# Down projection in seven block products: another order of the products, b11 loaded once, activation loads placed earlier in the program

## The chip, the cores and the metric

The kernel runs on one core of one Trainium2 chip. The metric is the device time of one execution in microseconds, the median of several runs of the same program. Each engine works through a queue of its own in order: TensorE (PE) multiplies, VectorE (DVE) and ScalarE (ACT) work on tiles, SyncE (SP) and GpSimd (POOL) issue the transfers here, POOL also adds a little. TensorE's clock can be throttled; the profile gives the clock that was granted.

## The reference

One encoder layer is applied to two requests of 256 and 512 tokens with the same weights; the kernel joins them to 768 rows. After three token mixers, a gated merge and an output projection comes the feed-forward part, in float32:

```python
    h2 = rmsnorm(x, ffn_norm_g[li])
    g, up = jnp.split(h2 @ w_gate_up[li], 2, axis=-1)
    x = x + (jax.nn.silu(g) * up) @ w_down[li]
    return x
```

`D_MODEL` is 1024 and `D_FF` 2816. The change touches only the last product, the down projection: hidden activations (768 x 2816) times `w_down` (2816 x 1024), added to the residual rows `x1` and stored.

## The kernel before

**Precision.** Each float32 operand is split in a rounded high part (written by ACT) and a low part (the rest, written by DVE). A product is three matmuls per 128-row step, `mm3` (L751 to L753): high by high, low by high, high by low. In the profile `whd` and `wld` are the parts of a weight tile, `dxh` and `dxl` those of an activation tile, and `split_evac` (L742, L743 without a scale, L745, L746 with one) writes them.

**Hidden activations.** The gate and up projections run in 11 blocks of 256 hidden columns. Block `fb` ends in an SBUF tile `fa` (128 x 1536 numbers, 0.786 MB), which SP stores to a DRAM tile `hid_scr[fb]` (L1425). The last such store, of block 10, is the last thing that the gate and up stage does.

**Seven products.** The down projection cuts rows and columns in halves: a11, a12, a21, a22 are the activations, with `A_(r, kh)` for row half `r` (384 rows each) and hidden half `kh`; b11, b12, b21, b22 are the quarters of `w_down`, `w_quarter(kh, f, g)` with `f` the half of the output columns. Seven products of sums of them give the four output blocks, in the order P1, P5, P6, P3, P7, P2, P4. P1 is a11 by b11, P2 a12 by b21. The hidden half is cut in granules `g` = 0 to 5 of two 128-row steps (the last has one). A product and a granule make an *item*, 42 in all, number 6 p + g. A full item is 3 row tiles x 2 steps x 3 matmuls = 18 matmuls, the last granule's 9; all are 693.

**Activation tiles.** `a_load` (L1712) fetches one half granule pair, 128 x 768 numbers (0.393 MB, half of that for granule 5), from `hid_scr` as `da<r><kh>_<g>`. The first `EARLY` = 3 lie in a pool of their own (`dae`) and are fetched during the gate and up stage. All others come from a pool that is opened when that stage's pools are closed and takes over their memory, so such a load waits for what is still read there, the last store of `fa` included. Sums of activations are made by DVE in place (L1757, `da` out of `da` and `da`, and `ds` for P3).

**Weight tiles.** A weight tile is 128 x 1024 numbers (0.524 MB, 0.262 for granule 5). Names in the profile: `dwr` are plain loads for P1, P3 and P2, with item numbers, in three buffers shared with the earlier stages; `dwt` are P7's, in three buffers; `dch0` to `dch5` are the *sum chain*, six tiles that stay. SP loads b11 into each, POOL adds b12 by an accumulating load (L1744) for P5, then b22 for P6, then b21 for P4, each after the splits of the item before have read the tile. P7's tile is b12 with b22 added.

**Order.** `w_fetch(i)` issues item i's weight load, `make(i)` its splits. The program runs `w_fetch` six and `make` two items ahead of the matmuls, but a list scheduler then places every instruction on its engine, so the written order is only the start. PE keeps four weight parts (`whd`, `wld`) and three activation parts (`dxh`, `dxl`). Products P1, P6, P7 and P4 gather in one set of three PSUM banks (`b`), P5 and P3, and then P2, in another (`d`). At a product's last granule DVE adds the three banks to `x1` (L1829), and after the last addition to a block SP stores it (L1831).

Of the kernel before, what the change touches and what calls it, by code (L numbers as in the profile page):

```python
# [626 lines left out]
def hybrid_block(ctx, tc, A, outs, consts):  # L627
# [20 lines left out]
    def uid(s):  # L648
        cnt[0] += 1
        return f"{s}_{cnt[0]}"  # L650
# [88 lines left out]
    def split_evac(hi, lo, src, scale=None):  # L739

        if scale is None:
            act.activation(hi, src, AF.Copy)  # L742
            v.tensor_tensor(out=lo, in0=src, in1=hi.bitcast(F32), op=sub)  # L743
        else:
            act.activation(hi, src, AF.Copy, scale=scale)  # L745
            v.scalar_tensor_tensor(out=lo, in0=src, scalar=scale, in1=hi.bitcast(F32), op0=mul, op1=sub)  # L746

    def mm3(ps, wh, wl, xh, xl, start, stop, more=False):

        kw = {"skip_group_check": True} if more else {}  # L750
        pe.matmul(ps, wh, xh, start=start, stop=False, **kw)  # L751
        pe.matmul(ps, wh, xl, start=False, stop=False, **kw)  # L752
        pe.matmul(ps, wl, xh, start=False, stop=stop, **kw)  # L753
# [43 lines left out]
    def bcast_load(pool, ap, n, name):  # L797
        t = pool.tile([128, n], F32, name=name)
        nc.sync.dma_start(t, ap.unsqueeze(0).to_broadcast([128, n]))
        return t  # L800
# [168 lines left out]
    D, P3 = {}, {}  # L969
    mrs2 = k1.tile([128, 4], F32, name="mrs2")  # L970
    with tc.tile_pool(name="nrm", bufs=1) as pool, tc.tile_pool(name="nrmg", bufs=1) as pg:
# [43 lines left out]
        g = bcast_load(pg, A["norm_mix_g"][0], 1024, "gmix")  # L1015
# [120 lines left out]
    for i, nme in enumerate(("diff_q_g", "diff_k_g")):  # L1136
        g = rp[:, 2, 64 * i : 64 * i + 64]
# [5 lines left out]
        s_ = slice(2 * i, 2 * i + 2)  # L1143
# [336 lines left out]
    with ExitStack() as c5:  # L1480
# [93 lines left out]
        g = fnp.tile([128, 1024], F32, name="gffn", bufs=1)  # L1574
# [117 lines left out]
    hid_store(0)  # L1692


    P1, P5, P6, P3, P7, P2, P4 = range(7)
    NG = NFB // 2 + 1

    def granule(kh, g):
        if g < NG - 1:
            return (NG - 1) * kh + g, 0, 2  # L1700
        return NFB - 1, kh, 1

    ITEMS = [(p, g) for p in range(7) for g in range(NG)]
    AHEAD, FETCH = 2, 6
    EARLY = 3
    de = ctx.enter_context(ExitStack())
    de.enter_context(tc.tile_pool(name="dgap", bufs=1, side="right")).tile([128, 16], F32, name="dgap")
    da_f = de.enter_context(tc.tile_pool(name="daf", bufs=3, side="right"))
# [3 lines left out]
    def a_load(q, g):  # L1712

        r, kh = q
        fb, m, n = granule(kh, g)
        early = q == (0, 0) and g < EARLY
        t = (da_e if early else DP["a"]).tile([128, 2, HT], F32, name=f"da{r}{kh}_{g}")[:, 0:n]
        nc.sync.dma_start(t, hid_scr[fb][:, m : m + n, HT * r : HT * r + HT])
        a_raw[q, g] = t

    def w_quarter(kh, f, g):
        fb, m, n = granule(kh, g)
        return wd[:, 2 * fb + m : 2 * fb + m + n, 512 * f : 512 * f + 512]

    def w_fetch(i):

        if i >= len(ITEMS):
            return
        p, g = ITEMS[i]
        n = granule(0, g)[2]  # L1730
        view = lambda t: t.rearrange("p (k c) -> p k c", k=2)[:, 0:n]
        if p in (P5, P6, P4):
            if p == P5:
                ch[g] = view(DP["ch"].tile([128, 1024], F32, name=f"dch{g}"))
                nc.sync.dma_start(ch[g], w_quarter(0, 0, g))
            t = ch[g]
            src, acc = None, {P5: (0, 1), P6: (1, 1), P4: (1, 0)}[p]
        else:
            t = view(DP["r"].tile([128, 1024], F32, name=f"dwt{i}", tag="dwt") if p == P7 else
                     W.praw.tile([128, W.HALF], F32, name=f"dwr{i}", tag="wr"))  # L1740
            src, acc = {P1: ((0, 0), None), P3: ((1, 1), None), P7: ((0, 1), (1, 1)), P2: ((1, 0), None)}[p]
            nc.sync.dma_start(t, w_quarter(*src, g))
        if acc:
            gp.dma_start(t, w_quarter(*acc, g), accum_op=add)  # L1744
        w_raw[i] = t

    def make(i):

        if i >= len(ITEMS):
            return  # L1750
        p, g = ITEMS[i]
        n = granule(0, g)[2]
        t = w_raw.pop(i)
        wh, wl = (x.rearrange("p (k c) -> p k c", k=2)[:, 0:n] for x in W.tiles(f"d{i}"))
        split_evac(wh, wl, t)
        A_ = lambda r, kh: a_raw[(r, kh), g]
        tt = lambda o, x, y, op: v.tensor_tensor(out=o, in0=x, in1=y, op=op)  # L1757
        sign = 0.5
        s_ = None if p == P1 else A_(1, 0)
        if p == P1:  # L1760
            x = A_(0, 0)
        elif p == P5:
            x = s_
            tt(x, x, A_(1, 1), sub)
        elif p == P6:
            x = s_
            tt(x, x, A_(0, 0), sub)
        elif p == P3:
            x = DP["t"].tile([128, 2, HT], F32, name=uid("ds4"), tag="ds4")[:, 0:n]
            tt(x, s_, A_(0, 1), add)  # L1770
        elif p == P7:
            x = s_
            tt(x, x, A_(1, 1), add)
            sign = -0.5
        else:
            x = A_(*((0, 1) if p == P2 else (1, 1)))
        xh, xl = (da_f.tile([128, 2, HT], F32R, name=uid("dx" + w), tag="dx" + w)[:, 0:n] for w in "hl")
        split_evac(xh, xl, x, sign)
        parts[i] = xh, xl, wh, wl

    def down_early():
        for i in range(3):
            w_fetch(i)
        for g in range(EARLY):
            a_load((0, 0), g)
        for i in range(AHEAD):
            make(i)

# [7 lines left out]
    with ExitStack() as c7:  # L1796
        for k, n in (("a", 1), ("ch", 1), ("t", 2), ("r", 3)):
            DP[k] = c7.enter_context(tc.tile_pool(name="down" + k, bufs=n))
        loads = [((0, 0), g) for g in range(EARLY, NG)]
        loads += [(q, g) for g in range(NG) for q in ((1, 0), (1, 1))] + [((0, 1), g) for g in range(NG)]  # L1800
        HOME = {P1: (0, 0, add), P5: (1, 1, add), P6: (0, 1, sub), P3: (0, 1, add), P7: (1, 1, sub),
                P2: (0, 0, add), P4: (1, 0, add)}
        acc = {}
        for _ in range(NG - EARLY):
            a_load(*loads.pop(0))
        for i in range(3, FETCH):
            w_fetch(i)
        for i, (p, g) in enumerate(ITEMS):
            for _ in range(3):
                if loads:  # L1810
                    a_load(*loads.pop(0))
            w_fetch(i + FETCH)
            make(i + AHEAD)
            bank = "b" if p in (P1, P6, P7, P4) else "d"
            if g == 0 and p in (P1, P5, P2):
                acc[bank] = [PS[bank].tile([128, 512], F32, name=uid("dn"), tag=bank) for _ in range(3)]
            ps = acc[bank]
            n = granule(0, g)[2]
            xh, xl, wh, wl = parts.pop(i)
            for t in range(3):  # L1820
                c = slice(128 * t, 128 * t + 128)
                for k in range(n):
                    mm3(ps[t], xh[:, k, c], xl[:, k, c], wh[:, k], wl[:, k],
                        g == 0 and k == 0 and p in (P1, P5, P2), g == NG - 1 and k == n - 1, p in (P6, P3, P7, P4))
            if g == NG - 1:
                r, f, op = HOME[p]
                for t in range(3):
                    o = x1[3 * r + t][:, 512 * f : 512 * f + 512]
                    v.tensor_tensor(out=o, in0=o, in1=ps[t], op=op)  # L1829
                    if p in (P3, P7, P2, P4):  # L1830
                        nc.sync.dma_start(os_[3 * r + t][:, 512 * f : 512 * f + 512], o)  # L1831
    de.close()
    x1ctx.close()
# [43 lines left out]
```

## Time and profile before

| | us |
|---|---|
| median of 3 runs | 1800.08 (1798.48 to 1800.41) |
| profiled execution | 1797.81 |
| its span, first to last instruction | 1796.0 |
| PE busy | 1742.0 (97%) |
| DVE busy | 1262.5 (70%) |
| ACT busy | 887.0 (49%) |
| POOL busy | 280.7 (16%) |

The page's 40 slices are 44.9 us each; the down projection takes the last four and a half of them. A row of the timeline reads: start, duration, engine, line, operation, output and inputs, shapes, and in brackets how long the engine stood idle before and what released it. SPq and POOL rows with DMA in them are issues, not transfers; several issues of a line are merged to one row with their count, which then spans from the first to the last. A row of the waits reads: who waited for whom, total us, times, longest. A row of the windows reads: stretch and its length, then busy time and count of PE, PE's weight loads, DVE, ACT and POOL, granted clock, busy share of the DMA engines, GB/s. DMA queue q1 carries what SP issues, q0 what POOL issues.

### The profile page before, as it was taken

To read this page: it belongs to the slowest core of one execution; us is meant where nothing else is said; L and a number is where in the kernel's file an instruction comes from. 1 tells how busy PE (TensorE), PEld (TensorE's weight loads), DVE (VectorE), ACT (ScalarE), POOL (GpSimd) and SP (SyncE) were. 2 spreads that over 40 slices of the span, in tenths; PEclk is the share of its full clock that TensorE was granted. 3 is DMA by queue.
4 is the path that set the end of the run, shared out by engine and by line. 5 is a ranking of instruction groups with operands and counts; after the bars stand their busy time and mean duration, and the time that the engine had idled before them with its cause. 6 is when DMAs were issued, how large, how long until landed. Compare 5 with 4: busy or idle time off the path is not lost.

```text
span 1796.0 us, 29428 instructions
## 1 busy us (share of the span) xinstructions
PE 1742.0 (97%) x11194; PEld 1608.4 (90%) x11194; DVE 1262.5 (70%) x2342; ACT 887.0 (49%) x1856; POOL 280.7 (16%) x300
## 2 busy tenths in 40 slices
PE   9999999999999999999989999999999999993999
PEld 8999988999999999999979888888899999982887
DVE  6665659699999588788865435443897777752964
ACT  6444444777676366787755333232444333321443
POOL 0000000000000101011100011000155555541200
PEclk9999999999999999999999999999999999996999
DMA  7223745664565566454853346331234323269851
GB/s 263 72 83 106 135 115 127 162 159 117 148 150 145 133 171 147 96 112 105 188 144 100 121 132 220 122 109 47 71 99 134 105 90 106 88 191 300 166 153 43
DMA packets 211165, 236.97 MB, mean 132 GB/s; under 512 B 57928, under 2 KB 173392, under 8 KB 211024
## 3 DMA queue, kind: packets, MB, share of 16 engines
q1 hardware_dynamic: 185584, 166.93, 30.8%
q0 software_dynamic: 24288, 65.02, 17.0%
q10 hardware_dynamic: 1152, 3.15, 0.5%
q8 instruction: 88, 1.44, 0.3%
q14 instruction: 53, 0.43, 0.1%
HBM read 168.66 MB, written 41.22 MB: 117 GB/s over the span
## 4 chain that ended last, share of the span: by engine, by line
PE 57%; DMA 4%; DVE 2%; issue 1%; SPq 1%; ACT 0%; POOL 0%; DVEq 0%; ACTq 0%; POOLq 0%
PE br L752 4%; PE br L751 4%; PE br L753 4%; PE gate L751 3%; PE gate L752 3%; PE up L752 3%; PE gate L753 3%; PE up L751 3%; PE up L753 3%; PE dn L753 3%; PE dn L751 3%; PE dn L752 3%; PE av L1311 2%; PE qk L752 2%; PE qk L751 2%; PE qk L753 2%
## 5 line engine op out<-in xcount | busy, mean ns | idle before, releaser
L595 ACT ACTIVATE wh<-wr 128x1024 fp32r<-128x1024 f32 x124 | 140.6, 1134 | 73.4 <-PE br L752 30.3
L601 DVE TENSOR_TENSOR wl<-wr,wh 128x1024 fp32r<-128x1024 f32 x82 | 108.4, 1323 | 84.4 <-ACT wh L595 82.6
L751 PE MATMUL gl<-Hhi,wh 128*128 128x256 f32 (+1 forms) x384 | 132.4, 345 | 2.3 <-ACT glt L1114 2.3
L753 PE MATMUL gl<-Hhi,wl 128*128 128x256 f32 (+1 forms) x384 | 129.0, 336 | 0.0
L752 PE MATMUL gl<-Hlo,wh 128*128 128x256 f32 (+1 forms) x384 | 128.7, 335 | 0.0
L751 PE MATMUL dn<-whd,dxh 128*128 128x512 f32 x231 | 90.8, 394 | 29.6 <-ACT dxh L745 29.6
L751 PE MATMUL qk<-wh,Hhi 128*128 128x256 f32 x384 | 108.7, 283 | 0.7 <-ACT V L1210 0.7
L752 PE MATMUL qk<-wl,Hhi 128*128 128x256 f32 x384 | 109.2, 284 | 0.0
L753 PE MATMUL qk<-wh,Hlo 128*128 128x256 f32 x384 | 108.4, 282 | 0.0
L599 POOL DMA_DIRECT2D wl<-wr x42 | 36.6, 872 | 453.9 <-ACT wl L598 440.5
L752 PE MATMUL dn<-wld,dxh 128*128 128x512 f32 x231 | 90.5, 392 | 0.0
L753 PE MATMUL dn<-whd,dxl 128*128 128x512 f32 x231 | 88.3, 391 | 1.2 <-DVE dxl L746 1.2
L751 PEld LDWEIGHTS gl<-Hhi,wh 128*128 128x128 f32 x384 | 72.3, 188 | 9.7 <-ACT glt L1114 2.7
L753 PEld LDWEIGHTS gl<-Hhi,wl 128*128 128x128 f32 x384 | 72.0, 187 | 8.0
L751 PEld LDWEIGHTS dn<-whd,dxh 128*128 128x128 f32 x231 | 43.9, 190 | 38.9 <-ACT dxh L745 30.0
L752 PEld LDWEIGHTS gl<-Hlo,wh 128*128 128x128 f32 x384 | 72.3, 188 | 7.2
L745 ACT ACTIVATE dxh<-da 128x768 fp32r<-128x768 f32 (+1 forms) x36 | 28.5, 792 | 93.9 <-PE dn L752 49.4
L751 PEld LDWEIGHTS qk<-wh,Hhi 128*128 128x128 f32 x384 | 73.1, 190 | 1.6 <-ACT V L1210 0.9
L1280 DVE TENSOR_REDUCE nm<-sc 128x1 f32<-128x512 f32 (+1 forms) x96 | 56.6, 598 | 25.5 <-PE sc L1275 24.5
L753 PEld LDWEIGHTS qk<-wh,Hlo 128*128 128x128 f32 x384 | 73.4, 191 | 0.3
L752 PEld LDWEIGHTS qk<-wl,Hhi 128*128 128x128 f32 x384 | 73.1, 190 | 0.6
L557 ACT ACTIVATE wh_S<-ws 128x512 fp32r<-128x512 f32 x70 | 41.1, 625 | 59.1 <-PE up L752 33.5
(478 smaller groups left out, 6046.6 us busy)
## 6 DMA issues: line engine op xcount, KB each, us to landing
wr<-in_w_in_dram SPq DMA_DIRECT2D x48, 512.0 KB, 4.5
wr<-in_w_gate_up_dram SPq DMA_DIRECT2D x44, 512.0 KB, 3.6
wl<-wr POOLq DMA_DIRECT2D x42, 512.0 KB, 5.4
wr<-in_w_branch_dram SPq DMA_DIRECT2D x24, 512.0 KB, 4.4
glr<-gl_scr POOLq DMA_DIRECT2D x24, 384.0 KB, 3.5
hid_scr<-fa SPq DMA_DIRECT2D x11, 768.0 KB, 6.5
wr<-in_w_mem_kv_dram SPq DMA_DIRECT2D x16, 512.0 KB, 3.6
wr<-in_w_in_dram SPq DMA_DIRECT2D x32, 256.0 KB, 4.3
```

The lines of the kernel that those rows point to most:

```text
L557: self.nc.scalar.activation(f(hi), src, AF.Copy)
L595: self.nc.scalar.activation(hi, r, AF.Copy)
L599: self.nc.gpsimd.dma_start(lo, r.bitcast(F32R), accum_op=ALU.add)
L601: self.sub.tensor_tensor(out=lo, in0=r, in1=hi.bitcast(F32), op=ALU.subtract)
L745: act.activation(hi, src, AF.Copy, scale=scale)
L751: pe.matmul(ps, wh, xh, start=start, stop=False, **kw)
L752: pe.matmul(ps, wh, xl, start=False, stop=False, **kw)
L753: pe.matmul(ps, wl, xh, start=False, stop=stop, **kw)
L1280: v.tensor_reduce(out=nm[:, m : m + 1], in_=ps, axis=AX.X, op=ALU.max, negate=True)
L1311: pe.matmul(po[:, 0:128], aT[:, 128 * k : 128 * k + 128], V[:, c0 // 128 + k, 128 * (h % 2) : 128 * (h % 2) + 128], start=(k == 0), stop=( ...
```

## The change

The products' order becomes P2, P1, P5, P6, P3, P7, P4. P1 no longer loads b11 into tiles of its own; it reads the sum chain's tile before anything is added to it, so b11 is read once and P5's addition of b12 follows P1's split. Four activation tiles, now of a12, are fetched early, where it was three of a11. The others are issued by item, seven items ahead, where a list gave three per item. P2's block is now stored after P1's addition.

```diff
-    P1, P5, P6, P3, P7, P2, P4 = range(7)
+    P2, P1, P5, P6, P3, P7, P4 = range(7)
...
-    AHEAD, FETCH = 2, 6
-    EARLY = 3
+    AHEAD, FETCH, LOAD = 2, 6, 7
+    EARLY = 4
+    NEW = {P2: ((0, 1),), P1: ((0, 0),), P5: ((1, 0), (1, 1))}
...
-        early = q == (0, 0) and g < EARLY
+        early = q == (0, 1) and g < EARLY
...
-        if p in (P5, P6, P4):
-            if p == P5:
+        acc = None
+        if p in (P1, P5, P6, P4):
+            if p == P1:
                 ch[g] = view(DP["ch"].tile([128, 1024], F32, name=f"dch{g}"))
                 nc.sync.dma_start(ch[g], w_quarter(0, 0, g))
+            else:
+                acc = {P5: (0, 1), P6: (1, 1), P4: (1, 0)}[p]
             t = ch[g]
-            src, acc = None, {P5: (0, 1), P6: (1, 1), P4: (1, 0)}[p]
...
-            src, acc = {P1: ((0, 0), None), P3: ((1, 1), None), P7: ((0, 1), (1, 1)), P2: ((1, 0), None)}[p]
+            src, acc = {P3: ((1, 1), None), P7: ((0, 1), (1, 1)), P2: ((1, 0), None)}[p]
...
+    def item_loads(i):
+        if i < len(ITEMS):
+            p, g = ITEMS[i]
+            for q in NEW.get(p, ()):
+                a_load(q, g)
...
-        for g in range(EARLY):
-            a_load((0, 0), g)
+        for i in range(EARLY):
+            item_loads(i)
...
-        loads = [((0, 0), g) for g in range(EARLY, NG)]
-        loads += [(q, g) for g in range(NG) for q in ((1, 0), (1, 1))] + [((0, 1), g) for g in range(NG)]
...
-        for _ in range(NG - EARLY):
-            a_load(*loads.pop(0))
+        for i in range(EARLY, LOAD):
+            item_loads(i)
...
-            for _ in range(3):
-                if loads:
-                    a_load(*loads.pop(0))
+            item_loads(i + LOAD)
...
-                    if p in (P3, P7, P2, P4):
+                    if p in (P1, P3, P7, P4):
```

Lines behind the change stand up to five lower in the kernel after: L1718 becomes L1719, L1744 L1747, L1757 L1760, L1829 L1834, L1831 L1836.

What the scheduler makes of it shows at three places. First SP's queue, from the last hidden store on, before:

```order
L1425 DMA hid_scr10_174<-fa_1786_17435 128x1536
L1742 DMA dwr19_18143<-in_w_down_dram 128x2x512
L1742 DMA dwr20_18172<-in_w_down_dram 128x2x512
L1718 DMA da00_3_17728<-hid_scr3_167 128x2x384
L1718 DMA da00_4_17730<-hid_scr4_168 128x2x384
L1718 DMA da00_5_17732<-hid_scr10_174 128x384
L1718 DMA da10_0_17740<-hid_scr0_164 128x2x384
L1718 DMA da11_0_17742<-hid_scr5_169 128x2x384
```

The same stretch of SP's queue after, with the six rows ahead of the store (`dwr24` to `dwr26` are P3's weights now, `dwt30` to `dwt32` P7's):

```order
L1737 DMA dch5_17899<-in_w_down_dram 128x512
L1745 DMA dwt30_18440<-in_w_down_dram 128x2x512
L1745 DMA dwr5_17740<-in_w_down_dram 128x512
L1745 DMA dwt31_18471<-in_w_down_dram 128x2x512
L1745 DMA dwt32_18502<-in_w_down_dram 128x2x512
L1425 DMA hid_scr10_174<-fa_1786_17435 128x1536
L1745 DMA dwr24_18270<-in_w_down_dram 128x2x512
L1745 DMA dwr25_18299<-in_w_down_dram 128x2x512
L1745 DMA dwr26_18328<-in_w_down_dram 128x2x512
L1719 DMA da01_4_17730<-hid_scr9_173 128x2x384
L1719 DMA da01_5_17732<-hid_scr10_174 128x384
L1719 DMA da00_0_17734<-hid_scr0_164 128x2x384
```

The `da` loads behind the store still stand in one piece (21 before, 20 after), now three `dwr` loads behind the store where there were two, and P1's a11 comes ahead of P5's pairs. Second, POOL's queue around its last work on `fa`, before:

```order
L1744 DMA dch0_17746<-in_w_down_dram 128x2x512
L1422 TENSOR_TENSOR fa_1786_17435<-fa_1786_17435,fs_1800_17577 128x384
L1744 DMA dch1_17784<-in_w_down_dram 128x2x512
L1422 TENSOR_TENSOR fa_1786_17435<-fa_1786_17435,fs_1801_17578 128x384
L1744 DMA dch2_17819<-in_w_down_dram 128x2x512
L1744 DMA dch3_17854<-in_w_down_dram 128x2x512
L1744 DMA dch4_17889<-in_w_down_dram 128x2x512
L1744 DMA dch5_17925<-in_w_down_dram 128x512
L1744 DMA dwt24_18284<-in_w_down_dram 128x2x512
L1744 DMA dwt25_18315<-in_w_down_dram 128x2x512
L1744 DMA dwt26_18346<-in_w_down_dram 128x2x512
L1744 DMA dch0_17746<-in_w_down_dram 128x2x512
```

POOL's queue after, from the same place on:

```order
L1422 TENSOR_TENSOR fa_1786_17435<-fa_1786_17435,fs_1800_17577 128x384
L1422 TENSOR_TENSOR fa_1786_17435<-fa_1786_17435,fs_1801_17578 128x384
L1747 DMA dwt30_18440<-in_w_down_dram 128x2x512
L1747 DMA dwt31_18471<-in_w_down_dram 128x2x512
L1747 DMA dwt32_18502<-in_w_down_dram 128x2x512
L1747 DMA dch0_17744<-in_w_down_dram 128x2x512
L1747 DMA dch1_17777<-in_w_down_dram 128x2x512
```

The six first accumulations into `dch` have moved behind P7's three, where each waits for P1's split of its tile. Third, DVE's queue in the kernel after, at the end of P1 (items 9 to 11) and the start of P5 (`da10` minus `da11` is P5's activation):

```order
L1760 TENSOR_TENSOR da10_2_17955<-da10_2_17955,da11_2_17957 128x768
L746 TENSOR_SCALAR dxl_1836_17996<-da00_4_17835,dxh_1835_17995 128x768
L1760 TENSOR_TENSOR da10_3_17986<-da10_3_17986,da11_3_17988 128x768
L743 TENSOR_TENSOR wld11_18023<-dch5_17899,whd11_18022 128x512
L1760 TENSOR_TENSOR da10_4_18017<-da10_4_18017,da11_4_18019 128x768
L1760 TENSOR_TENSOR da10_5_18048<-da10_5_18048,da11_5_18050 128x384
L746 TENSOR_SCALAR dxl_1838_18027<-da00_5_17865,dxh_1837_18026 128x384
```

In the kernel before the last low part of P1 (item 5) stands ahead of all subtractions in DVE's queue:

```order
L746 TENSOR_SCALAR dxl_1823_17862<-da00_5_17732,dxh_1822_17861 128x384
L1757 TENSOR_TENSOR da10_0_17740<-da10_0_17740,da11_0_17742 128x768
L1757 TENSOR_TENSOR da10_1_17744<-da10_1_17744,da11_1_17778 128x768
L1757 TENSOR_TENSOR da10_2_17780<-da10_2_17780,da11_2_17782 128x768
L746 TENSOR_SCALAR dxl_1825_17898<-da10_0_17740,dxh_1824_17897 128x768
```

So the subtractions for granules 4 and 5 have come to stand ahead of P1's last low part.

More of the change, by code (lines that the diff above doesn't have):

```diff
@@ L1758, in make @@
         sign = 0.5
-        s_ = None if p == P1 else A_(1, 0)
+        s_ = A_(1, 0) if p in (P5, P6, P3, P7) else None
         if p == P1:
```

## Prediction

> **What bounds the kernel now.** The page first: TensorE decides, and the clock's row shows one hole late in the run.
>
> ```profile
> span 1796.0 us, 29428 instructions
> PE 1742.0 (97%) x11194; PEld 1608.4 (90%) x11194; DVE 1262.5 (70%) x2342; ACT 887.0 (49%) x1856; POOL 280.7 (16%) x300
> PEclk9999999999999999999999999999999999996999
> ```
>
> PE is busy for 97% of the span, so an edit can win time only in the 3% where PE stands still. The waits of the last 400 us name nearly all of it, and PE's timeline in the down projection gives the times:
>
> ```profile
> PE dn L751 <- ACT dxh L745: 29.6, 1, 29.6
> PE dn L753 <- DVE dxl L746: 1.2, 1, 1.2
> 1601.82 0.39 PE L751 MATMUL dn<-whd,dxh 128*128 128x512 f32 x1
> 1613.88 0.39 PE L753 MATMUL dn<-whd,dxl 128*128 128x512 f32 x1
> 1643.82 0.79 PE L751 MATMUL dn<-whd,dxh 128*128 128x512 f32 x1 [29.55 <-ACT dxh L745]
> 1657.54 0.50 PE L753 MATMUL dn<-whd,dxl 128*128 128x512 f32 x1 [1.15 <-DVE dxl L746]
> 1791.90 0.39 PE L753 MATMUL dn<-whd,dxl 128*128 128x512 f32 x1
> ```
>
> The first three items (54 matmuls) run from 1601.82 to 1613.88, so a matmul takes 0.2275 us and a full item of 18 takes 4.10 us. Then PE waits 29.55 us for the fourth item's activations, and 1.15 us once later. All 693 matmuls at 0.2275 us would end at 1759.5; the last starts at 1791.90. The difference, some 32 us, is all that this stage has to give: the two waits and about 1.6 us of slow clock after the first.
>
> Who is late? SP's queue, the reader ACT, and the landing of the last store:
>
> ```profile
> 1597.85 3.28 SPq L1735 DMA_DIRECT2D dch<-in_w_down_dram  x6
> 1607.83 0.34 SPq L1425 DMA_DIRECT2D hid_scr<-fa  x1
> 1608.92 8.74 SPq L1742 DMA_DIRECT2D dwr<-in_w_down_dram  x2
> 1631.11 29.00 SPq L1718 DMA_DIRECT2D da<-hid_scr  x21
> 1642.92 0.84 ACT L745 ACTIVATE dxh<-da 128x768 fp32r<-128x768 f32 x1 [25.43 <-DMA da<-hid_scr]
> DMA to landing us min/median/max: 11.7/15.9/23.2
> ```
>
> The last hidden block's store goes out at 1607.83 and lands 23.2 us later, at 1631.0. The first `da` load that is not an early one goes into memory which that store still reads, so it is issued at 1631.11, and ACT has it at 1642.92. Why so slow? The rates say it:
>
> ```profile
> 1601.80:1606.00 4.20, 4.20 (x21) 3.46 (x20) 1.78 (x2) 1.06 (x1) 2.68 (x4) 1.00 1.05 384
> 1608.00:1614.00 6.00, 6.00 (x28) 4.87 (x26) 0.89 (x1) 0.00 (x0) 4.36 (x4) 1.00 1.08 263
> 1616.00:1642.00 26.00, 0.00 (x0) 0.00 (x0) 1.92 (x2) 1.49 (x2) 3.62 (x3) 0.51 1.10 267
> 1648.00:1657.00 9.00, 8.39 (x38) 6.61 (x36) 4.12 (x6) 4.18 (x6) 0.00 (x0) 1.00 1.06 379
> 1684.00:1696.00 12.00, 12.00 (x54) 9.95 (x53) 9.06 (x11) 4.62 (x6) 4.51 (x4) 1.00 0.98 160
> ```
>
> The last two columns are the DMA share and GB/s. The engines are full (1.05 to 1.10) all through the stall. Plain loads alone move 379 to 384 GB/s, accumulating loads alone 160 (1684 to 1696), both together 263 to 267. By queue, for 1610 to 1630 (packets, MB, share):
>
> ```profile
> q0 software_dynamic: 1280, 2.47, 66.6%
> q1 hardware_dynamic: 1279, 2.97, 42.8%
> ```
>
> They take turns packet by packet (1280 against 1279), so while POOL's queue (q0) has work, SP's (q1) gets about 131 GB/s instead of 384. POOL's work in the stall is this:
>
> ```profile
> 1603.32 1.22 POOL L1744 DMA_DIRECT2D dch<-in_w_down_dram  x1 [3.23 <-ACT whd L742]
> 1606.82 5.55 POOL L1744 DMA_DIRECT2D dch<-in_w_down_dram  x4
> 1614.20 1.20 POOL L1744 DMA_DIRECT2D dwt<-in_w_down_dram  x1 [1.84 <-DMA dwt<-in_w_down_dram]
> 1625.08 1.70 POOL L1744 DMA_DIRECT2D dch<-in_w_down_dram  x1
> ```
>
> A check of this reading: from 1600 to 1608 SP's queue moves 8 x 0.384 = 3.07 MB. Up to the end of the store it has 6.03 MB (`dch` 5.5 x 0.524, three `dwt` and `dwr18` at 0.524, `dwr5` 0.262, the store 0.786). The other 2.96 MB at 0.131 take 22.6 us: 1630.6. The trace has 1631.0. The `da` load behind it (`dwr19`, `dwr20` and itself, 1.44 MB) takes 11.0 us: 1642.1; ACT starts at 1642.92.
>
> **The change, part by part.**
>
> *One more early item.* P2 comes first and four of its activation tiles are loaded early, not three: PE runs to 1601.82 + 72 x 0.2275 = 1618.2 before it can stall. Gain 4.1 us. These four loads stand right behind the stores of blocks 5 to 8, whose landing SP awaits. Before has two such places, behind blocks 1 and 2; one is this, with block 8's place below it and PE's waits of 1270 to 1640:
>
> ```profile
> 1374.25 0.34 SPq L1425 DMA_DIRECT2D hid_scr<-fa  x1
> 1378.89 0.53 SPq L1718 DMA_DIRECT2D da<-hid_scr  x1
> 1386.38 3.02 SPq L539 DMA_DIRECT2D wr<-in_w_gate_up_dram  x2
> ...
> 1547.86 0.34 SPq L1425 DMA_DIRECT2D hid_scr<-fa  x1
> 1559.14 0.37 SPq L539 DMA_DIRECT2D wr<-in_w_gate_up_dram  x1
> ...
> PE gate L751 <- ACT fhi L742: 0.7, 1, 0.7
> ```
>
> SP waits 4.6 us, but the `wr` load queued behind it goes out 11 us after a store anyway (1559.14), since its buffer comes free then. PE waits nowhere there. Cost 0; uncovered it would be 4.6 us, four times.
>
> *POOL's first six accumulations leave the stall.* `dch` is now P1's weight as it comes, so it is added to only after P1's split has read it. Of ten accumulations in the stall (5.5 + 3 + 1 of 0.524 MB, 4.98 MB) there remain `dwt30` to `dwt32` and those of `dch0` and `dch1`: 2.62 MB. Six plain loads of b11 (2.88 MB) go too.
>
> When does q1 lose its full rate now? POOL's first accumulation waits for `dwt30`, that is for 2.88 + 0.52 = 3.41 MB of q1: 1600 + 8.9, about 1610 with the semaphore. Before, POOL issued at 1603.32 and the rate fell from 384 to 263 between 1606 and 1608, some 4 us later; so q0 starts at 1614. By then q1 has moved 14 x 0.384 = 5.38 of the 5.50 MB that end with the store, which lands at 1615 instead of 1631. Now `dwr24` to `dwr26` and the first `da01` load stand ahead: 0.12 + 1.57 + 0.39 = 2.1 MB at 0.131, 16.0 us, to 1630.0. q0 is busy until 1614 + 2.62 / 0.131 = 1634, so this stretch is shared throughout. With the 0.8 us by which the check above was short, and the 0.9 us from ACT to PE, PE restarts at 1631.7 instead of 1643.82: gain 12.1 us. The stall is 13.5 us, still long enough for the clock to fall (0.51 in the stall before), so the slow restart stays.
>
> The bounds: with POOL's data from 1611, the store ends at 1620.8 and PE restarts at 1637.5; with q0 empty at 1626 (late P1 splits), PE restarts at 1629.1.
>
> [...]
>
> *A new wait, in DVE's row.* P5's subtractions for granules 4 and 5 stand ahead of the low part of P1's last item (DVE rows above), so that item now waits for `da11_5`. From 1630.0 SP's queue has 0.20 + 2.16 + 4.32 = 6.68 MB to bring. Shared to 1634: 0.5 MB. Alone until `dch2` can be added to (item 4 ends about 1637.4, two splits and 4 us of POOL: 1645): 4.2 MB. The last 2.0 MB shared: 15 us, to 1660. PE needs the item at 1631.7 + 1.6 + 4.1 + 2.05 + 5 x 4.1 = 1660. Behind the landing come a subtraction and the low part, which for a half granule take
>
> ```profile
> 1714.43 0.55 DVE L1757 TENSOR_TENSOR da<-da,da 128x384 f32<-128x384 f32 x1
> 1715.18 0.56 DVE L746 SCALAR_TENSOR_TENSOR dxl<-ds,dxh 128x384 fp32r<-128x384 f32 x1 [0.20 <-ACT dxh L745]
> ```
>
> 0.55 us each, and the 0.8 us from the check above lies between landing and use. That makes 1.9 us; with some waiting between engines I take 2.4 us, between 0 (unshared) and 6 (a quarter slower). The old 1.15 us wait was for P5's first subtraction, right after the stall; it goes, as that has a whole product of time now.
>
> *P4 right behind P7 in the same banks.* Before, P2 stood between. P4's first matmul now waits for DVE to empty tile 0. Tile 0 ends six matmuls (1.4 us) before P7 does; before, behind P2, DVE took
>
> ```profile
> 1768.52 0.69 DVE L1829 TENSOR_TENSOR x<-x,dn 128x512 f32<-128x512 f32 x1 [1.94 <-PE dn L753]
> ```
>
> 0.69 us, with no delay. PE's new order takes tile 0 of three items first, so tiles 1 and 2 have time. Cost 0; with a split of 1.2 us in front, 0.6 us.
>
> *Loads seven items ahead.* All later `da` loads stand in one piece in SP's row, as before: nothing of its own.
>
> Sum: 4.1 + 12.1 + 1.2 - 2.4 = 15.0 us. The span goes from 1796.0 to 1781.0, the profiled time from 1797.8 to 1782.8. The median shown is 2.3 us above the profiled run, so I forecast 1800.1 - 15.0 = 1785.1. About 0.2% (3.6 us) is what a measurement of this kernel can tell from no change.
>
> **The rivals.**
>
> *The stall nearly closes (0.11).* Accumulations at half of the full rate, 192 GB/s, would bring the first `da01` load in 10.9 us; PE restarts at 1626.6 and the DVE wait goes: 17.2 + 4.1 + 1.2 = 22.5 us, 1777.6. If q0 came later than the load, 5.5 us: 1772. For it: the shared rate was seen only with POOL's queue always filled. Against: 263 to 267 GB/s held for 34 us. [...]
>
> *The store stays late (0.07), so the change doesn't do what it says.* SP's queue still holds nine half-megabyte loads ahead of the store, 5.50 MB against 6.03. Were they, not POOL, the cause, the store would land near 1631 again, and 4.1 + 1.2 - 2.4 = 2.9 us remain: 1797.2. Against: 384 GB/s while POOL is silent.
>
> *Slower: DVE's queue is the new stall (0.06).* If SP's queue has only 131 GB/s all the way from 1630, the 6.68 MB take 51 us, `da11_5` lands at 1681 and P1's last item waits 22 us: 17.4 - 22 = -4.6, so 1804.7. It decides below 6.68 / 47.4 = 141 GB/s. For it: DVE takes its row in order, and the shared rate is 131. Against: POOL has 2.62 MB until 1634, then nothing until P1's next splits, and 379 GB/s is what a lone queue gets.
>
> **How the numbers follow.** The forecast has 0.76. Its own bounds: restart at 1637.5 and 6 us in DVE give 5.6 us (1794.5); restart at 1629.1 and no DVE wait give 20 us (1780). The range 1777 to 1794 takes in the first rival and leaves out the other two. Faster by over 0.2%: 0.76 + 0.11 = 0.87; within: 0.07; slower: 0.06.
>
> **What would show it.** Right: one PE wait of 10 to 19 us with ACT `dxh` as its cause, from about 1618; the store landing within 8 to 13 us; 384 GB/s until about 1614, then about 263; a PE wait of 1 to 4 us for `dxl` near 1660; no wait at P4. Wrong: the store landing after 20 us (POOL wasn't the cause), a stall under 8 us (sharing is milder), or a DVE wait above 10 us.

## The result, and the profile after

| | before | after |
|---|---|---|
| median of 4 runs each | 1799.28 us | 1784.98 us |
| lowest and highest | 1797.97 to 1800.41 | 1783.40 to 1785.10 |
| profiled execution, its span | 1797.81, 1796.0 | 1785.03, 1783.3 |

The ratio of after to before is 0.9919, with a 95% interval of 0.9902 to 0.9936; the medians are 14.3 us apart, the two spans 12.7 us. The forecast was 1785.1.

First the page of after: the span, the engines' busy time, and the granted clock in 40 slices.

```profile
span 1783.3 us, 29404 instructions
PE 1746.8 (98%) x11194; PEld 1612.8 (90%) x11194; DVE 1263.0 (71%) x2342; ACT 887.1 (50%) x1856; POOL 280.2 (16%) x300
PEclk9999999999999999999999999999999999998999
```

The hole in the clock's row stands in the same slice and is shallower, 8 where before had 6. PE's waits of 1270 to 1784 show what is left in it (who waited for whom, total us, times, longest):

```profile
PE dn L751 <- ACT dxh L745: 10.9, 1, 10.9
PE dn L753 <- DVE dxl L746: 3.6, 1, 3.6
PE gate L751 <- ACT fhi L742: 0.7, 1, 0.7
```

PE's timeline has the places, and the rows where the matmuls are back at full pitch:

```profile
1629.20 0.79 PE L751 MATMUL dn<-whd,dxh 128*128 128x512 f32 x1 [10.85 <-ACT dxh L745]
1634.06 0.40 PE L751 MATMUL dn<-whd,dxh 128*128 128x512 f32 x1
...
1662.35 0.79 PE L753 MATMUL dn<-whd,dxl 128*128 128x512 f32 x1 [3.64 <-DVE dxl L746]
1668.36 0.40 PE L752 MATMUL dn<-wld,dxh 128*128 128x512 f32 x1
```

The wait for the first late activations fell from 29.55 to 10.85 us. The wait for `dxl` grew from 1.15 to 3.64 us and has another place, the end of P1. Up to the rows at 1634.06 and 1668.36 the clock is slow (0.50 and 0.52 granted): 4.86 us for 11 matmuls (2.50 us at 0.2275 us each) and 6.01 us for 14 (3.19 us). They cost 2.36 and 2.82 us. Before had one such stretch, 1643.82 to 1647.39 (0.50 granted) with 8 matmuls, which cost 1.75 us.

These pieces make up the difference: waits 30.7 to 14.5 us (16.2 less), slow clock 1.75 to 5.2 us (3.4 more), together 12.8 us less, where the spans differ by 12.7. Ahead of the down projection nothing changed in these two traces: its first matmul starts at 1601.82 in both. From the first matmul's start to the last one's it takes 190.1 us before and 176.9 us after; behind the last matmul after needs 0.4 us more to its end.

SP's queue in after:

```profile
1605.05 0.34 SPq L1425 DMA_DIRECT2D hid_scr<-fa  x1
1606.40 5.97 SPq L1745 DMA_DIRECT2D dwr<-in_w_down_dram  x3
1615.07 30.11 SPq L1719 DMA_DIRECT2D da<-hid_scr  x20
```

POOL's queue, its first accumulation (the releaser in the bracket is inferred):

```profile
1611.07 1.22 POOL L1747 DMA_DIRECT2D dwt<-in_w_down_dram  x1 [7.35 <-PE dn L753]
```

ACT's timeline, where it has the first late tile:

```profile
1628.30 0.84 ACT L745 ACTIVATE dxh<-da 128x768 fp32r<-128x768 f32 x1 [8.87 <-DMA da<-hid_scr]
```

The last hidden store goes out at 1605.05, and at 1615.07 SP may issue the load that waits for it: 10 us, where before took 23. The first `da` load then takes 13 us more. The windows say why the one is fast and the other slow (last three columns: granted clock, DMA share, GB/s):

```profile
1614.00:1616.00 2.00, 2.00 (x11) 1.65 (x10) 0.60 (x1) 1.06 (x1) 1.50 (x2) 1.00 1.05 390
1616.00:1618.00 2.00, 2.00 (x11) 1.61 (x9) 0.62 (x1) 0.00 (x0) 0.84 (x1) 1.00 1.11 269
1628.00:1630.00 2.00, 0.80 (x2) 0.71 (x3) 0.82 (x1) 0.84 (x1) 0.00 (x0) 0.50 1.10 247
1660.00:1665.00 5.00, 2.65 (x6) 2.15 (x7) 3.73 (x5) 0.00 (x0) 1.20 (x1) 0.63 0.03 8
```

390 GB/s until 1616, then 269 and less, with the engines full (1.05 to 1.11): POOL's accumulations begin to share at 1616, after the store has landed. At 1660 to 1665 the DMA engines are idle (0.03) and the clock is down to 0.63: the transfers of this stretch are over, and PE still stands until 1662.35. DVE's timeline shows what it waits for:

```profile
1658.93 0.96 DVE L1760 TENSOR_TENSOR da<-da,da 128x768 f32<-128x768 f32 x1 [4.67 <-DMA da<-hid_scr]
1661.27 0.56 DVE L1760 TENSOR_TENSOR da<-da,da 128x384 f32<-128x384 f32 x1 [1.38 <-DMA da<-hid_scr]
1661.74 0.55 DVE L746 SCALAR_TENSOR_TENSOR dxl<-da,dxh 128x384 fp32r<-128x384 f32 x1
```

DVE stands 4.67 and 1.38 us before P5's two last subtractions, for tiles that PE needs a whole product later, and only then writes the low part (1661.74) for which PE stands.

### The profile page after: what moved, and what is told of

Same layout as the page of the kernel before. It is cut to its first block, busy times and chain, and to the rows that moved or that the text cites. A ratio compares the mean times of both kernels' runs of the same rounds, so it can differ in the third digit from the quotient of the medians.

```text
span 1783.3 us, 29404 instructions
## 1 busy us (share of the span) xinstructions
PE 1746.8 (98%) x11194; PEld 1612.8 (90%) x11194; DVE 1263.0 (71%) x2342; ACT 887.1 (50%) x1856; POOL 280.2 (16%) x300
## 4 chain that ended last, share of the span: by engine, by line
PE 56%; DMA 5%; DVE 1%; issue 1%; ACT 0%; POOL 0%; SPq 0%; DVEq 0%; ACTq 0%; POOLq 0%
PE br L752 4%; PE br L751 4%; PE br L753 4%; PE gate L751 3%; PE gate L752 3%; PE gate L753 3%; PE up L752 3%; PE up L751 3%; PE up L753 3%; DMA da<-hid_scr 2%; PE dn L753 2%; PE dn L752 2%; PE dn L751 2%; PE av L1311 2%; PE qk L752 2%; PE qk L751 2%
## 5 line engine op out<-in xcount | busy, mean ns | idle before, releaser
L745 ACT ACTIVATE dxh<-da 128x768 fp32r<-128x768 f32 (+1 forms) x36 | 28.5, 791 | 87.5 <-PE dn L752 58.3
L558 DVE TENSOR_TENSOR wl_S<-ws,wh_S 128x512 fp32r<-128x512 f32 x70 | 58.4, 858 | 14.8 <-ACT wh_S L557 14.8
```

Of the source, the lines that this page charges most:

```text
L558: self.nc.vector.tensor_tensor(out=f(lo), in0=src, in1=f(hi).bitcast(F32), op=ALU.subtract)
```

## The experiments

**The theory.** The last store and the first late `da` load lie in SP's queue, and that queue is slow for as long as POOL's accumulating loads share the DMA engines with it. The change took six of these accumulations out of the stall. **The rivals:** SP's own bytes made the store late; the order of the products gives the gain by itself; the fourth early item does.

All kernels ran beside the kernel before (its medians in these comparisons: 1799.35, 1799.65 and 1799.69). The stages ahead differ by up to 5 us between profiled executions, so places in different traces are counted from the first matmul of the down projection.

In the table the stall is PE's wait for the first activations that were not loaded early, and the restart is its end. "None" says that PE doesn't stand there; p7_late and store_first wait later, as told below.

| kernel | median, us | ratio to before (95%) | stall, us | restart, us after the start |
|---|---|---|---|---|
| before | 1799.3 | 1 | 29.55 | 42.0 |
| after | 1785.0 | 0.9919 (0.9902 to 0.9936) | 10.85 | 27.4 |
| three_early | 1785.9 | 0.9920 (0.9906 to 0.9935) | 14.97 | 27.4 |
| own_b11 | 1795.1 | 0.9972 (0.9963 to 0.9982) | 25.12 | 41.6 |
| before_four | 1801.5 | 1.0014 (1.0005 to 1.0023) | 24.89 | 41.4 |
| before_accs_late | 1805.6 | 1.0036 (1.0023 to 1.0048) | 15.66 | 28.1 |
| subs_behind | 1780.6 | 0.9897 (0.9882 to 0.9912) | 11.95 | 28.5 |
| p7_accs_late | 1772.8 | 0.9856 (0.9842 to 0.9871) | 3.88 | 20.4 |
| p7_late | 1775.2 | 0.9862 (0.9844 to 0.9880) | none | none |
| p7_late_subs_behind | 1768.5 | 0.9830 (0.9815 to 0.9845) | none | none |
| store_first | 1775.2 | 0.9860 (0.9844 to 0.9877) | none | none |
| own_b11_plain | 1790.2 | 0.9948 (0.9929 to 0.9967) | 18.72 | 35.2 |

**1. The fourth early item alone, taken from after (three_early) and given to before (before_four).**

```diff
-    EARLY = 4
+    EARLY = 3
```

(and 3 to 4 in the kernel before).

> The kernel after with EARLY = 3 instead of 4; nothing else is changed. Theory (SP's queue and POOL's accumulations set the restart, not the number of early items): PE runs 54 matmuls and stalls from 1614; the first late da load is one tile earlier in the queue but lands at the same time, so PE restarts near 1629 as in after (1629.20) and the stall is about 15 us. The wait for dxl at P1's last item (3.64 us in after) shrinks below 1 us, since PE gets there 4.1 us later while da11_5 lands about 1 us later, and the slow clock behind that wait goes too. Sum: -4.1 + 3.3 + 2.4, about the same time as after, within 2.5 us (1783 to 1788). Rival (the fourth early item is worth its full 4.10 us, as the prediction's sum has it): 1789.1.

> The kernel before with EARLY = 4 instead of 3. Theory: PE stalls from 1618 instead of 1614, the restart stays near 1643, and the wait for P5's first activations (1.15 us in before) grows to 2 to 4 us since PE gets there 4.1 us sooner: 0.5 to 3 us faster than before. Rival (an early item is worth 4.1 us wherever it is): 4.1 us faster, 1795.2.

PE's waits in three_early, and then PE's timeline in before_four:

```profile
PE dn L751 <- ACT dxh L745: 15.0, 1, 15.0
PE dn L753 <- DVE dxl L746: 0.7, 1, 0.7
```

```profile
1647.10 0.79 PE L751 MATMUL dn<-whd,dxh 128*128 128x512 f32 x1 [24.89 <-ACT dxh L745]
1657.55 0.69 PE L751 MATMUL dn<-whd,dxh 128*128 128x512 f32 x1 [2.30 <-ACT dxh L745]
1674.97 0.50 PE L753 MATMUL dn<-whd,dxl 128*128 128x512 f32 x1 [1.80 <-DVE dxl L746]
```

The restart stays where it is in both pairs (27.4 and 27.4 us; 42.0 and 41.4). In three_early the stall is 4.1 us longer than in after, the later wait 2.9 us shorter, and the clock stays up behind it: 1785.93 (1781.71 to 1787.83) against 1784.98, no difference that can be told. In the two profiled executions the stage is even 1.7 us shorter without the item (175.3 against 176.9 us from first to last start). In before the item isn't worth 4.1 us either: 4.7 us of stall less, 2.95 us of later waits more, and a second slow stretch, 1657.55 to 1661.20. It came out 0.1% slower, where 0.5 to 3 us faster was expected, so even the theory was too kind to it. In the profiled executions the stage takes 190.2 us with the item and 190.1 without, so what makes the medians 2.1 us apart isn't shown. An early item lets PE run ahead of loads that set the pace; PE then waits further on.

**2. The new order with the old chain (own_b11).** P1 loads b11 into tiles of its own, and b12 is added to the chain at once.

```diff
-        if p in (P1, P5, P6, P4):
-            if p == P1:
+        if p in (P5, P6, P4):
+            if p == P5:
...
-            src, acc = {P3: ((1, 1), None), ...
+            src, acc = {P1: ((0, 0), None), P3: ((1, 1), None), ...
```

> The kernel after with the old chain: P1 loads b11 into tiles of its own and the chain's tiles get b11 and at once b12 added, as in before. Order of the products and the four early items stay. Theory: POOL's six accumulations are back in the stall and share with SP's queue from about 1608, so the last hidden store lands at 1626 to 1631, PE restarts at 1640 to 1644 and the stall is 22 to 26 us; the time is 1793 to 1799, so the order of the products by itself is worth at most the early item. Rival (the new order of products gives the gain, by itself): store at 1615, 1785 to 1787.

SP's queue in own_b11:

```profile
1613.05 0.34 SPq L1425 DMA_DIRECT2D hid_scr<-fa  x1
1634.77 10.18 SPq L1719 DMA_DIRECT2D da<-hid_scr  x7
```

The store lands 21.7 us after its issue again (10.0 in after), PE restarts 41.6 us after the start, and of the gain 4.2 us are left. So the chain, not the order, carries 10 of after's 14 us. This edit brings back POOL's six accumulations and SP's six loads of b11 together; the next one tells them apart.

**3. The kernel before with nothing but POOL's six accumulations put off (before_accs_late).** All of SP's loads stay. The copy `marks[0]` is queued on POOL and reads the low part of the fourth item's activations.

```diff
+            marks.append(gp.tensor_copy(out=mark[:, 0:1], in_=xl[:, 0, 0:1].bitcast(F32)))
...
+            with tc.issue_after(marks[0].ins):
+                while late:
+                    t, src = late.pop(0)
+                    gp.dma_start(t, src, accum_op=add)
```

> The kernel before; only POOL's six first accumulations (b12 into the chain, for P5) are queued behind a one-column copy on POOL that reads the low part of the fourth item's activations, so they start after PE's restart. SP's loads are all still there, 6.03 MB up to the store's end. Theory (POOL's traffic slowed SP's queue): SP's queue keeps 384 GB/s up to about 1615, the store lands at 1614 to 1618 instead of 1631 and PE restarts at 1623 to 1631, a stall of 9 to 17 us in place of 29.55. Afterwards the accumulations run beside P5's da pairs at about 131 GB/s each, where P5 needs 0.79 MB per 4.1 us, so 5 to 15 us come back as waits at P5: total 0 to 15 us faster than before. Rival (SP's own bytes made the store late): store at 1629 or later, restart at 1641 or later, no faster.

SP's queue in before_accs_late:

```profile
1608.81 0.34 SPq L1425 DMA_DIRECT2D hid_scr<-fa  x1
1610.16 6.04 SPq L1743 DMA_DIRECT2D dwr<-in_w_down_dram  x3
1619.35 38.06 SPq L1719 DMA_DIRECT2D da<-hid_scr  x21
```

PE's waits in the same kernel:

```profile
PE dn L752 <- DVE wld L743: 16.9, 1, 16.9
PE dn L751 <- ACT dxh L745: 15.7, 1, 15.7
PE dn L751 <- ACT whd L742: 1.7, 1, 1.7
```

DVE's timeline ahead of the longest of them:

```profile
1657.97 1.43 DVE L1760 TENSOR_TENSOR da<-da,da 128x384 f32<-128x384 f32 x2 [1.64 <-DMA da<-hid_scr]
1663.70 3.49 DVE L743 TENSOR_TENSOR wld<-dch,whd 128x1024 fp32r<-128x1024 f32 x3
```

The mechanism is as the theory has it, and the rival falls: with all of before's bytes in SP's queue the store lands after 10.5 us instead of 23, and PE restarts 28.1 us after the start instead of 42.0. But the time, expected 0 to 15 us faster, is 6.3 us slower. The accumulations now run beside P5's `da` loads, and PE waits 16.9 us for a weight's low part that DVE writes only behind sums for which tiles have not landed. My bound of 5 to 15 us for what comes back was too small: 18.6 us of waits and another slow restart (0.50 granted from 1665 to 1670). So in this kernel putting b12's addition off gains nothing by itself; with P2 ahead of P1 and P1 between the early items and b12's use, it gains 10 us. Part of the loss is DVE's row, in which sums stand ahead of the low part that PE needs. Whether the old order with that row mended would have gained something wasn't run.

**4. DVE's row (subs_behind).** P5's subtractions are kept in written order on DVE.

```diff
-            tt(x, x, A_(1, 1), sub)
+            tc.keep_in_program_order(tt(x, x, A_(1, 1), sub))
```

> The kernel after; only P5's subtractions on DVE are kept behind everything that is written before them on DVE, so none of them stands ahead of the low part of P1's last item. Theory (the 3.64 us wait and the slow clock behind it come from DVE's row order, not from a late load that PE itself needs): the wait for dxl near 1662 goes, and with it about 2.5 us of slow clock; 4 to 6 us faster than after, 1779 to 1781. Rival (P5's pairs land late anyway, and the wait only moves to P5's own items): within 1.5 us of after.

In subs_behind PE waits for nothing in the down projection but this:

```profile
PE dn L751 <- ACT dxh L745: 11.9, 1, 11.9
```

The wait for `dxl` and the slow clock behind it are gone: 1780.64 against 1784.98, 4.3 us, at the low end of 4 to 6; the first stall was 1.1 us longer in this execution. The place of the subtractions in DVE's row was the cause, and P5 itself lost nothing: no wait appears there.

**5. What is left of the stall: accumulations or bytes? (p7_late, p7_accs_late, p7_late_subs_behind)** POOL's three accumulations for P7, and the three loads ahead of them, still lie in after's stall. p7_late keeps the loads in written order (the accumulations follow them), p7_accs_late only the accumulations, on top of subs_behind.

```diff
-            nc.sync.dma_start(t, w_quarter(*src, g))
+            ld = nc.sync.dma_start(t, w_quarter(*src, g))
+            if p == P7:
+                tc.keep_in_program_order(ld)
```

```diff
-            gp.dma_start(t, w_quarter(*acc, g), accum_op=add)
+            ac = gp.dma_start(t, w_quarter(*acc, g), accum_op=add)
+            if p == P7:
+                tc.keep_in_program_order(ac)
```

> The kernel after; only P7's weight loads on SP are kept in the order in which they are written, so dwt30 to dwt32 and their three accumulations leave the stall. Theory: up to the store's end SP's queue has 3.9 MB instead of 5.5, at 384 GB/s it lands about 10 us after SP's queue got its full rate (near 1610 to 1611 on the clock of after's trace); two dwr loads and the first da load, 1.44 MB, take 4 to 6 us more, so PE restarts within 2 us of the end of its 72 early matmuls (1618.2): the stall of 10.85 us nearly vanishes. But P1 now runs 11 us sooner, its accumulations start by 1621 and share from there, and P5's pairs (the last of them 6.7 MB behind the first load) can't land before 1645 to 1660, while P1's last item is due at 1645: the wait for dxl grows from 3.6 to 5 to 15 us. Sum: 0 to 10 us faster than after, likeliest 6 (1779). Rival (with POOL silent early, nothing is late any more): no wait for dxl above 4 us, 13 us or more faster.

> The kernel subs_behind (after with P5's subtractions kept behind P1's splits); besides, only POOL's three accumulations for dwt30 to dwt32 are kept in written order, so POOL is silent in the stall. SP's loads stay, 5.5 MB up to the store's end and 2.1 MB from there to the first late da load. Theory (what is left of the stall, 11.95 us in subs_behind, is both bytes and sharing): at 384 GB/s throughout the store lands where it did (about 10 us after its issue, POOL's data began only then), but the 2.1 MB behind it take 5.5 us instead of 13, so PE's stall is 3 to 5 us and the time 7 to 9 us below subs_behind (1772 to 1774); the other 4 us, which p7_late_subs_behind has too, are the three loads' own 1.57 MB. Rival (three accumulations cost little once the store has landed, the bytes ahead are what counts): a stall of 9 us or more, within 3 us of subs_behind.

> The kernel after with both edits: P7's weight loads in written order, and P5's subtractions kept behind P1's splits on DVE. Theory: no stall at 1618 (under 2 us) and no wait for dxl at P1's last item; P5's pairs are needed one by one, 0.79 MB per 4.1 us from 1649, and they land in time or a few us late. 12 to 18 us faster than after: 1767 to 1773. Rival (P5's pairs come no faster than 131 GB/s beside POOL's accumulations and PE waits for each): gain under 8 us.

PE's one wait in the down projection in p7_late, and then the one in p7_accs_late:

```profile
PE dn L753 <- DVE dxl L746: 5.3, 1, 5.3
```

```profile
PE dn L751 <- ACT dxh L745: 3.9, 1, 3.9
```

In p7_late the stall is gone, DVE's wait has grown to 5.3 us, and 9.8 us are gained. In p7_accs_late the stall is 3.88 us and the gain on subs_behind 7.9 us, as expected: that is the sharing, with all of SP's bytes still there. The 3.88 us that are left are about what the 1.57 MB of the three loads take (an estimate: 4.1 us at 384 GB/s), and p7_late_subs_behind, which moves these loads too, has no stall and is 4.2 us faster. So the rival, SP's own bytes, has a part in what remains, the smaller one.

With both edits PE waits nowhere in the down projection, as expected. The page of p7_late_subs_behind, its engines and its clock:

```profile
PE 1739.9 (99%) x11194; PEld 1607.6 (91%) x11194; DVE 1264.4 (72%) x2342; ACT 887.7 (50%) x1856; POOL 280.4 (16%) x300
PEclk9999999999999999999999999999999999999999
```

And the view of the tile `dn`, the rows of the high-by-high and the high-by-low matmuls (count, then min, median and longest in ns, first and last start):

```profile
L751 PE MATMUL dn<-whd,dxh x231: 387/389/390, 1604.6 to 1761.0; 128*128 128x512 f32 x116
L753 PE MATMUL dn<-whd,dxl x231: 388/389/398, 1605.0 to 1761.5; 128*128 128x512 f32 x116
```

No matmul is longer than 398 ns, and the stage takes 156.9 us from first to last start, where 693 matmuls at 0.2275 us are 157.7 us to the end of the last. At 1768.54 us (1767.75 to 1770.83) this kernel beats both, and in this stage PE's own work is all that is left.

**6. The store ahead of b11 (store_first).** Besides, the loads of b11 into the chain are kept in written order, behind the store.

```diff
-                nc.sync.dma_start(ch[g], w_quarter(0, 0, g))
+                tc.keep_in_program_order(nc.sync.dma_start(ch[g], w_quarter(0, 0, g)))
```

> The kernel after with both edits of p7_late_subs_behind, and b11's loads into the chain (dch) also kept in written order, so SP's queue has only four loads for P2's last items ahead of the last hidden store, and the da loads come ahead of dch. Theory: the store lands within 6 us of its issue, the first late da load within 6 more, before PE is out of its early items: no stall at all. dch still comes in time for P1 (0.52 MB per 4.1 us). As p7_late_subs_behind or up to 2 us better: 1766 to 1772. Rival (SP waits in its queue for the store, and b11 comes late behind it): PE waits for whd or wld at P1's first items, 3 us or more, and it is slower than p7_late_subs_behind.

SP's queue around the store:

```profile
1603.85 0.34 SPq L1425 DMA_DIRECT2D hid_scr<-fa  x1
1604.93 0.38 SPq L1745 DMA_DIRECT2D dwr<-in_w_down_dram  x1
1607.49 2.41 SPq L1719 DMA_DIRECT2D da<-hid_scr  x4
```

What DVE waited for later, and PE's one wait in the down projection:

```profile
1640.86 0.69 DVE L743 TENSOR_TENSOR wld<-dch,whd 128x512 fp32r<-128x512 f32 x1 [6.48 <-ACT whd L742]
PE dn L753 <- DVE dxl L746: 4.1, 1, 4.1
```

The store lands in 3.6 us and there is no stall, as expected; but it is 6.6 us slower than p7_late_subs_behind, as the rival said, by a longer way. The last b11 tile comes late behind `da` tiles and beside accumulations, ACT and DVE stand 6.8 and 6.5 us for it, DVE then works almost without a pause up to PE's wait of 4.13 us, at P5's second item, for a low part. That the one leads to the other is read from the trace, not shown by a run of its own. Here the earliest store isn't the best one: it has only to land before PE runs out.

**7. Is it the adding? (own_b11_plain)**

```diff
-            gp.dma_start(t, w_quarter(*acc, g), accum_op=add)
+            gp.dma_start(t, w_quarter(*acc, g), **({} if p == P5 else {"accum_op": add}))
```

> The kernel own_b11; the six loads that POOL issues for P5 in the stall bring the same b12 to the same tiles at the same place in its queue, but without adding (so b11 is left out of the chain from P5 on, and the output isn't the reference's). Theory (it is the adding that makes POOL's packets slow, and SP's queue, which takes turns with them, slow too): both queues together move 350 GB/s or more until POOL's sixth load is done, SP's half is about 190 instead of 131, the store lands some 7 us sooner than in own_b11, and PE's stall is 13 to 18 us instead of 25.1; 7 to 12 us faster than own_b11. Rival (two queues in turn are slow whatever they carry): 263 GB/s, a stall of 24 us or more, the time of own_b11.

The DMA view of 1612 to 1625, in most of which both queues are filled, in own_b11 and then in own_b11_plain (queue: packets, MB, time as a share of 16 engines):

```profile
DMA packets 1821, 3.53 MB, mean 271 GB/s; under 512 B 106, under 2 KB 106, under 8 KB 1820
q0 software_dynamic: 801, 1.56, 64.8%
q1 hardware_dynamic: 1019, 1.95, 44.2%
```

```profile
DMA packets 1854, 4.92 MB, mean 379 GB/s; under 512 B 161, under 2 KB 161, under 8 KB 1853
q0 software_dynamic: 869, 3.03, 63.8%
q1 hardware_dynamic: 984, 1.88, 39.8%
```

Without the adding both together move 379 instead of 271 GB/s, so the adding loads, with the smaller packets that they come in, are what is slow. Its price lies elsewhere than I had it, though. SP's queue gets no more than before (1.88 MB against 1.95): the queues take turns by packets (in after, 1618 to 1628, POOL's and SP's are 718 and 716), and POOL's packets carry 3.5 KB in own_b11_plain, where nearly all are plain, and 1.95 KB in own_b11, in about the same time (153 and 168 ns). In own_b11's window SP's packets are more, 1019 against 801: up to about 1613.3 the rate is still 334 to 384 GB/s, as for SP's queue alone. From 1614 to 1622 both together move 261 (own_b11) and 388 GB/s. POOL is simply done sooner with its six loads. That gave 4.9 us and a stall of 18.7 us, where 7 to 12 us and 13 to 18 us were expected.

The loads seven items ahead have no run of their own: with `LOAD` at 4 or 10 every engine's row holds the same instructions in the same order, so there is nothing to time.

## Why the prediction was right, step by step

- **POOL's first six accumulations.** Right in mechanism; forecast 12.1 us, measured 14.6 (restart at 1629.20, not 1631.7). own_b11 and before_accs_late show the cause from both sides. The mis-sized term is the moment when sharing begins: 1616, not 1614. POOL's first accumulation went out at 1611.07 (forecast 1610) and its data took longer to start: its first packets come after 1615. So SP's queue moved about 0.5 MB more (an estimate: 2 us at 384 GB/s instead of the 115 that it had from 1618 to 1628). The store landed at 1615.07, forecast 1615.
- **One more early item, 4.1 us.** Right where it was booked, at the stall, and wrong as a term of the sum: three_early has the same time without it. The wait at P1's last item is there because PE arrives 4.1 us sooner. The two terms, 4.1 and -2.4, belonged to one row.
- **The new wait in DVE's row.** The right place and cause (subs_behind). Forecast 2.4 us, measured 3.64. What the step left out is the clock: behind the second wait PE was slow again (0.52 granted), which cost 2.8 us, and the first restart was 0.6 us slower than before's. The sentence "so the slow restart stays" counted one such stretch where there are two.
- **The old wait of 1.15 us** went, and **P4 behind P7** cost nothing: PE's waits hold no row for either. **The early loads behind the stores** cost nothing: the only wait of the gate and up stage is the 0.7 us that before has too. SP issued them 4.6 to 6.6 us after the stores. (Before has three such loads, not two; the first follows the store of block 0.) **The placement of the loads** changes no row.
- **The sum.** 15.0 forecast, 12.7 in the profiled executions, 14.3 between the medians. The restart gave 2.5 us more than forecast; DVE's wait (1.2) and the slow clock (3.4) took 4.6 back. That the median hit the forecast to 0.1 us is luck: these errors of the steps partly cancel, and what is left, 2.3 us by the spans, was made up by two things. Before's profiled execution was 1.5 us faster than the median of its four runs here (1797.81 against 1799.28) while after's was at its median, and that median of before came out 0.8 us under the 1800.1 from which the forecast started.
- **The rivals.** The stall that nearly closes: no, sharing held at 245 to 269 GB/s; without the adding both queues together moved 379 (own_b11_plain, 271 in own_b11). The store that stays late: no. DVE's queue as the new stall: it was one, at 3.64 us instead of 22, and p7_late shows it growing to 5.3 us once PE arrives sooner.

## What to carry to other kernels

When a load waits for a store, look at who else is in the DMA engines during that store: here a second queue took turns with the first and left it only as many packets as it moved itself (716 against 718 from 1618 to 1628 in after, 1279 against 1280 from 1610 to 1630 in before). At the 384 GB/s that SP's queue had alone (before, 1601.8 to 1606) it would move 5.0 MB in 13 us, an estimate. From 1612 to 1625 it moved 1.88 MB in own_b11_plain, 3.1 MB less, where POOL's queue moved 3.03 MB. It fell as far short in own_b11, 3.0 MB, where POOL's accumulating loads moved only 1.56 MB, so slow packets on one queue cost the other more than their own bytes. An engine that works its row in order should not meet an operation for later work, whose data is still on its way, ahead of one that TensorE needs now (in after DVE stood 4.67 and 1.38 us before two such sums); pinning one such group brought 4 us here, and pinning three loads that a scheduler had drawn forward brought 12 more. Before a head start is booked as a gain, look for the next thing that PE would reach too early.

## What the runs showed of the hardware

- In own_b11 the accumulating loads on POOL's queue moved packets of 1.95 KB at 168 ns each (64.8% of 16 engines over 13 us, 801 packets), in own_b11_plain the loads there, nearly all plain, packets of 3.5 KB at 153 ns (63.8%, 869 packets). Per byte the time is about twice as long with the adding. SP's packets in own_b11's window, 1.9 KB, took 90 ns each (44.2%, 1019 packets).
- A short wait cost most of its own length again in two places: 1.8 us behind the wait of 2.30 us (before_four), 2.8 us behind that of 3.64 (after). Behind the waits of 0.69 (three_early), 1.15 (before) and 1.80 us (before_four) PE went on at full pitch; behind those of 2.30 us and more it ran at about 0.43 us a matmul, in stretches of 3.6 us (before) to 6.0 us (after). In p7_accs_late the slow stretch doesn't even begin at once, as PE's timeline shows:

```profile
1624.24 0.50 PE L751 MATMUL dn<-whd,dxh 128*128 128x512 f32 x1 [3.88 <-ACT dxh L745]
1624.58 0.40 PE L752 MATMUL dn<-wld,dxh 128*128 128x512 f32 x1
1625.29 0.56 PE L751 MATMUL dn<-whd,dxh 128*128 128x512 f32 x1
1628.94 0.62 PE L753 MATMUL dn<-whd,dxl 128*128 128x512 f32 x2
```

  PE runs the first four matmuls in 1.05 us, three of them 0.24 us apart, and only then slows, until 1628.94. The stretches of 3.6, 4.9 and 6.0 us in before and after stand behind waits of 29.55, 10.85 and 3.64 us: there the longer wait didn't bring the longer stretch. What sets their length, and what delays the onset here, isn't shown.
